# Input rows through another buffer ring, first sums' slabs loaded earlier, and two first-gate products in general PSUM banks

## The chip, the cores and the metric

The kernel runs on one core of a Trainium2 chip. The core has five instruction queues that run at their own pace and meet through semaphores: TensorE (PE, matrix products, which accumulate in eight PSUM banks), VectorE (DVE), ScalarE (ACT), GpSimd (POOL) and SyncE (SP, which here only issues transfers). Each queue executes in order. Sixteen DMA engines move data between main memory and the on-chip SBUF. The metric is the device time of one execution, in microseconds (us); lower is better.

## The reference, cut to what matters

One layer of a streaming encoder over 2048 prompt rows and 64 sample rows of width 1024, all in fp32. The first half of the layer makes two mixers, a convolution module and a chunk-band attention. The part that matters here begins behind them:

```python
merged = jax.nn.sigmoid(g_conv) * conv_out + jax.nn.sigmoid(g_attn) * attn_out
x = x + gt1 * (merged @ p['w_o'])

h2 = rms_norm(x, p['norm2_g']) * (1 + sc2) + sh2
gate, up = jnp.split(h2 @ p['w_ffn_in'], 2, axis=-1)
x = x + gt2 * ((jax.nn.silu(gate) * up) @ p['w_ffn_out'])
```

The FFN has 22 groups of 128 hidden columns; `w_ffn_in` holds the 22 gate groups and then the 22 up groups.

## The kernel before, in words

**Products.** An fp32 operand is kept as a high and a low part. For weights, ACT copies the slab into `whi` (rounded), and DVE or POOL subtracts, `wlo = slab - whi` ("the split"). A product is then three passes on PE: high by high, low by high, high by low (`mm3`).

**Blocks.** The second phase (merge, output projection, residual, FFN) goes over three blocks of tokens, `CBLOCKS`: 0 to 576, 576 to 1344, 1344 to 2112. The tokens of a block are cut into two halves of columns (288 in block 0, 384 in the others), and its FFN input `h2`, transposed, is held as four quarters b11, b21, b12, b22 (row half, column half of the tokens) and combinations t1 to t4 of them.

**Seven products.** The gate and the up weights of a group are combined in the manner of Strassen, so that seven quarter products do the work of eight. The weights' side needs four sums s1 to s4 of quarters of the gate's slab and of the up's slab. POOL makes them (`operand`, tiles named `ws`, a ring of four in SBUF), in the first block only, and each is stored to main memory (`sum_d`) for the blocks that follow. The names `g`, `u` in `operand` are the two slabs. `presum` makes a gate's sums ahead of their split. The splits of these weights run in the order of use.

**The start of a block's FFN.** Behind the output projection (PSUM tiles `pw`) runs `residual`, once per tile of 128 tokens (of 64 for the sample rows), as a generator that a planner steps: it loads the input rows `x_t` (two halves of 512 columns, in the ws ring too), adds them (`x1`), stores x1, takes the sum of squares on ACT, the root `r` on POOL, scales (`xn`, ACT), transposes on PE into `pw` or `pt` banks, scales the columns on DVE and ACT, and then makes the copies and differences: b11 and b21 for tokens of the first half, and for tokens of the second half t3, b22, t2, t1 and t4, each as a high copy on ACT and a low difference on DVE.

While the second half's tokens go through this, PE has work that needs the first half alone: the first five gates (`EARLY = 5`) use a plain product of b11 and b21 for the gate of the first half (`first(f)` and `second(f)`, ACT and DVE then make the silu of it, tiles `early` and `tg`). The first four products go into the banks that have the tags y0, z0, y1, z1; four more banks have the tag gp and serve in turn. Then follow the 22 groups (`up`), with products named by their weights' side, s1 to s4, a12, a22, and their tokens' side, t1 to t4, b21, b22; the early part of each ends in the tiles `u` and `v` on DVE.

**What sets the order.** `Stream` keeps a rough clock per engine as the program is written out, and calls deferred steps when its clock of PE has reached them: loads, splits, sums, generators. `Weights` walks a list of keys in the order of use (`weight_order`); what must come from main memory is listed in `items`, and `due` is the order of loading. A slab goes into the first of the classes wst (three buffers), wup and wfo that has room; a new load is issued on SP when a buffer comes free (`drop`, `left`). `get` makes what is not yet there. The framework then orders each engine's instructions, so that the order of PE around `first` and `second` is not literally the source's.

**Three lines hold the sums back.** In block 0 `W.hold` is true from the merge until the residual's column scalings are done; while it is, `presum` makes no sums, and `available` gives no key of kind `up` to the splits. And `presum` looks only at the key that is next to be split, `i = len(self.ready)`; as long as first-gate slabs (`fi`) are still to be split, it makes nothing.

In the profile nearly all instructions carry line 102, that of `Meter.run`, a helper which counts every operation; so the rows are told apart by the names of tiles. L1748 is the loading of x_t, L1767 the store of x1, L375 the load of a slab, L423 the store of a sum, L501 the store of a split first-gate slab.

Of the kernel before, what the change touches and what calls it, by code (L numbers as in the profile page):

```python
# [8 lines left out]
F32 = mybir.dt.float32  # L9
# [7 lines left out]
P = 128  # L17
D = 1024
# [9 lines left out]
FFN = 2816  # L28
# [235 lines left out]
class Weights:  # L264
# [5 lines left out]
    def __init__(self, engines, pool, dram, stream, keys, source, staging, held, kept):  # L270
# [2 lines left out]
        self.pool, self.dram, self.keys, self.source = pool, dram, keys, source  # L273

        self.staging, self.held, self.reach = staging, held, 0
        self.sum_pool, self.sum_d, self.sums, self.hold, self.landed = None, None, {}, 0, {}
        self.behind = nullcontext

        self.room, self.leaving = {"wst": 1, "wup": 0, "wfo": 0}, {"wst": 0, "wup": 0, "wfo": 0}
        times, raws = {}, {}  # L280
# [7 lines left out]
        for i, key in enumerate(keys):  # L288
            n = times[key] = times.get(key, 0) + 1
# [31 lines left out]
        self.due = {kind: [] for kind in self.tags}  # L321
        for i, key in enumerate(self.items):
            self.due[self.kind(key)].append(i)
        self.load_on("")

    @staticmethod
# [116 lines left out]
    def presum(self):  # L443

        i = len(self.ready)
        if not self.hold and i in self.first and all(self.landed.get(j, 1e18) <= self.stream.load["pe"] for j in self.need[i]):
            for f, op in self.keys[i][1:]:
                if op[0] == "s":
                    self.operand(f, op)
# [60 lines left out]
    def available(self):  # L510
        i = len(self.ready)
        if i >= len(self.keys):
            return False
        if i in self.need:
            if not self.there(i) or self.hold and self.keys[i][0] == "up":
                return False
            return True
        return self.keys[i] in self.stored

    def fill(self):  # L520
# [91 lines left out]
def streaming_layer(ctx: ExitStack, tc: tile.TileContext, I, O):  # L612
    nc = tc.nc
    stream = Stream()
    pe, dve, act, gps = (
        Meter(e, n, stream) for e, n in ((nc.tensor, "pe"), (nc.vector, "dve"), (nc.scalar, "act"), (nc.gpsimd, "pool"))
    )
    x_p, x_s = I["x_prompt"][0], I["x_sample"][0]
# [9 lines left out]
    def rows(prompt, sample, t, n):  # L628
        return prompt[t - SMP : t - SMP + n] if t >= SMP else sample[t : t + n]
# [137 lines left out]
    wk = p1.enter_context(tc.tile_pool(name="wk", bufs=1))  # L767
# [353 lines left out]
    def quarter(name, i, dtype=F32R, shape=(P, 4, CW // 2)):  # L1121

        return (wc, wk)[i].tile(list(shape), dtype, tag=f"half{i}", name=name, bufs=(4, 10)[i])
# [492 lines left out]
    W = Weights((nc.sync, act, dve, gps), wpool, dram, stream, list(weight_order()), source, 3, 5, lambda key: key[0] in KEPT)  # L1616
# [70 lines left out]
    wk = ctx.enter_context(tc.tile_pool(name="wk2", bufs=1))  # L1687
# [54 lines left out]
    def residual(pp, t, n, gt1, a, half, hs, free, last, i):  # L1742


        which = int(t < SMP)
        x_t = [wk.tile([P, 512], F32, tag="ws", name="x_t", bufs=4) for _ in range(2)]
        for j in range(2):
            nc.sync.dma_start(x_t[j][:n], rows(x_p, x_s, t, n)[:, 512 * j : 512 * j + 512])  # L1748
        yield
        x1 = token_row("x1")  # L1750
        for j in range(2):
            f = slice(512 * j, 512 * j + 512)
# [6 lines left out]
        for j in range(2):  # L1759
            f = slice(512 * j, 512 * j + 512)  # L1760
# [33 lines left out]
        for c, e, o in ((0, min(n, half - a), a), (max(0, half - a), n, max(0, a - half))):  # L1794
# [16 lines left out]
            t = pts[1][:, :, c:e]  # L1811
# [24 lines left out]
    for s, (lo, hi) in enumerate(CBLOCKS):  # L1836
# [4 lines left out]
        for i, (c0, c1) in enumerate(chunks):  # L1841
# [8 lines left out]
            if not groups:  # L1850
# [1 line left out]
                    gt1[which] = gt_row(0, which)  # L1852
                hs = {x: [quarter(x, 0) for _ in range(2)] for x in ("b11", "b21")}
                hs["rows"] = hs["columns"] = len(tiles)
            W.hold = not s

            def free():
                if xs:
# [9 lines left out]
            ws = {}  # L1868
# [44 lines left out]
        def bank(tag):  # L1913
            return bank_of(tag, "ps")[:, :half]
# [313 lines left out]

        def first(f):
            w = W.get(("fi", f * P))  # L2230
            x = bank(("y0", "z0", "y0", "z1", "y1")[f])
            product(x, [t[:, :4] for t in w], "b11", True, False)
            copy(early[f][0][:, :half], x)
            begin[f] = w, x
# [8 lines left out]
            step(f)  # L2243
        while hs["columns"]:
            turns.step(turns.gens[0])
        W.hold = False
        W.presum()
        if not s:
            W.begin_last()
# [19 lines left out]
        ws = [W.get(("fo", f)) for f in last]  # L2269
# [40 lines left out]
```

## Time and profile before

| | before |
|---|---|
| runs (us) | 2962.74, 2967.28, 2965.84 |
| median (us) | 2965.84 |
| the profiled execution's own time (us) | 2961.11 |
| its span (us) | 2959.3 |
| mean granted clock of TensorE | 0.996 |
| PE busy | 2888.9 us, 98% |
| DVE, ACT, POOL busy | 69%, 46%, 39% |

The profiled execution is one of several and took 4.7 us less than the median. Its span begins with the first and ends with the last instruction that the trace shows; 1.8 us lie around it. Times in the trace are counted from the start of the span. A row of the timeline gives the start, the duration, the engine, line and operation, then the tiles as out<-in with their shapes, the count of merged instructions, and in brackets the idle time of the engine before the first of them with the one that ended it. [...] The start of block 0's FFN lies at 1280 to 1360 us, that of block 1 at about 1830 to 1870, that of block 2 at about 2460 to 2500.

### The profile page before, as it was taken

To read this page: it belongs to the slowest core of one execution; us is meant where nothing else is said; L and a number is where in the kernel's file an instruction comes from. 1 tells how busy PE (TensorE), PEld (TensorE's weight loads), DVE (VectorE), ACT (ScalarE), POOL (GpSimd) and SP (SyncE) were. 2 spreads that over 40 slices of the span, in tenths; PEclk is the share of its full clock that TensorE was granted. 3 is DMA by queue.
4 is the path that set the end of the run, shared out by engine and by line. 5 is a ranking of instruction groups with operands and counts; after the bars stand their busy time and mean duration, and the time that the engine had idled before them with its cause. 6 is when DMAs were issued, how large, how long until landed. Compare 5 with 4: busy or idle time off the path is not lost.

```text
span 2959.3 us, 44845 instructions
## 1 busy us (share of the span) xinstructions
PE 2888.9 (98%) x16181; PEld 2583.0 (87%) x16181; DVE 2048.2 (69%) x3664; ACT 1365.8 (46%) x2453; POOL 1153.5 (39%) x745
## 2 busy tenths in 40 slices
PE   7999899999999999989999999999999999999999
PEld 5899777787888788879999999999999999999998
DVE  5897687668857885477777746676666547566666
ACT  3345633661465357464443345444444345444442
POOL 1101310111011102444466452366666742465767
PEclk9999999999999999999999999999999999999999
DMA  9989889988986888885444776332333975333333
GB/s 320 315 288 301 279 279 300 284 262 275 304 277 224 282 254 280 272 290 167 151 153 147 257 256 230 103 115 94 112 121 108 323 231 185 97 98 109 115 107 125
DMA packets 467724, 628.05 MB, mean 212 GB/s; under 512 B 36276, under 2 KB 314664, under 8 KB 467501
## 3 DMA queue, kind: packets, MB, share of 16 engines
q1 hardware_dynamic: 453600, 606.11, 63.1%
q10 hardware_dynamic: 13901, 19.08, 1.8%
q8 instruction: 127, 2.08, 0.3%
q14 instruction: 96, 0.79, 0.1%
HBM read 476.53 MB, written 148.54 MB: 211 GB/s over the span
## 4 chain that ended last, share of the span: by engine, by line
PE 82%; DVE 8%; DMA 4%; ACT 2%; POOL 2%; issue 2%; SPq 0%; ACTq 0%; POOLq 0%; DVEq 0%
PE ps L102 53%; PE pd L102 15%; PE pw L102 6%; DVE y L102 2%; PE sc L102 2%; PE po L102 2%; PE ptp L102 2%; DVE wlo L102 1%; PE pt L102 1%; PE pa L102 1%; ACT whi L102 1%; DMA tg<-g_d 1%; POOL wlo L102 1%; DVE pw L102 1%; DMA kk<-k_d 1%
## 5 line engine op out<-in xcount | busy, mean ns | idle before, releaser
L102 PE MATMUL ps<-t,whi 128*128 128x384 f32 (+1 forms) x2112 | 503.0, 322 | 9.0 <-ACT t L102 5.0
L102 POOL TENSOR_TENSOR wlo<-wst,whi 128x1024 fp32r<-128x1024 f32 (+1 forms) x159 | 363.6, 2297 | 249.4 <-ACT whi L102 227.1
L102 ACT ACTIVATE whi<-wst 128x1024 fp32r<-128x1024 f32 (+1 forms) x263 | 256.8, 979 | 321.0 <-PE ps L102 118.7
L102 PE MATMUL ps<-b,whi 128*128 128x384 f32 (+1 forms) x1584 | 380.6, 325 | 6.9 <-DVE early L102 3.6
L102 PEld LDWEIGHTS ps<-t,whi 128*128 128x128 f32 x2112 | 367.7, 188 | 17.0 <-ACT t L102 5.2
L102 DVE SCALAR_TENSOR_TENSOR y<-u,wd,y 128x512 f32<-128x512 f32 (+1 forms) x480 | 369.0, 773 | 6.3
L102 PE MATMUL ps<-hh,whi 128*128 128x512 f32 (+2 forms) x992 | 361.5, 364 | 0.0
L102 DVE TENSOR_TENSOR acc<-acc,pd 128x512 f32<-128x512 f32 x482 | 322.3, 684 | 49.6 <-PE pd L102 47.1
L102 PE MATMUL ps<-hl,whi 128*128 128x512 f32 (+2 forms) x992 | 345.6, 348 | 0.0
L102 PE MATMUL ps<-hh,wlo 128*128 128x512 f32 (+2 forms) x992 | 345.0, 348 | 0.0
L102 PE MATMUL ps<-t,wlo 128*128 128x384 f32 (+1 forms) x1056 | 339.2, 321 | 0.8 <-POOL wlo L102 0.7
L102 PE MATMUL pd<-whi,hid 128*128 128x512 f32 x912 | 297.0, 390 | 0.1
L102 PEld LDWEIGHTS ps<-b,whi 128*128 128x128 f32 x1584 | 277.8, 189 | 13.1 <-DVE early L102 4.5
L102 POOL TENSOR_TENSOR r<-t,mhalf 128x1 f32<-128x1 f32 (+2 forms) x68 | 84.4, 1243 | 445.3 <-DVE t L102 435.0
L102 PE MATMUL ps<-b,wlo 128*128 128x384 f32 (+1 forms) x792 | 256.6, 324 | 0.0
L102 ACT ACTIVATE pr<-pr,sm 128x640 f32<-128x640 f32 (+3 forms) x272 | 200.1, 747 | 111.0 <-DVE sm L102 108.5
L102 PEld LDWEIGHTS ps<-hh,wlo 128*128 128x128 f32 x992 | 186.7, 188 | 21.7
L102 PEld LDWEIGHTS ps<-hh,whi 128*128 128x128 f32 x992 | 187.1, 189 | 18.6 <-issue 1.6
L102 PEld LDWEIGHTS pd<-whi,hid 128*128 128x128 f32 x912 | 171.1, 188 | 35.6 <-ACT hid L102 0.7
L102 PEld LDWEIGHTS ps<-hl,whi 128*128 128x128 f32 x992 | 187.5, 189 | 15.5 <-issue 1.4
L102 PEld LDWEIGHTS ps<-t,wlo 128*128 128x128 f32 x1056 | 198.1, 188 | 2.4 <-POOL wlo L102 1.3
L102 PE MATMUL ps<-cin,whi 128*128 128x384 f32 (+2 forms) x768 | 184.0, 325 | 3.3 <-DVE o_p L102 1.4
(228 smaller groups left out, 6234.5 us busy)
## 6 DMA issues: line engine op xcount, KB each, us to landing
whi<-w_din_h SPq DMA_DIRECT2D x72, 512.0 KB, 6.8
wlo<-w_din_l SPq DMA_DIRECT2D x72, 512.0 KB, 7.4
wst<-sum_d SPq DMA_DIRECT2D x132, 256.0 KB, 2.9
wfo<-in_w_ffn_out SPq DMA_DIRECT2D x64, 512.0 KB, 3.4
wmod<-in_w_ada SPq DMA_DIRECT2D x46, 512.0 KB, 9.0
sum_d<-ws SPq DMA_DIRECT2D x88, 256.0 KB, 2.1
wst<-in_w_ffn_in SPq DMA_DIRECT2D x84, 256.0 KB, 3.2
wst<-in_w_in SPq DMA_DIRECT2D x40, 512.0 KB, 7.6
```

The costliest lines, as they stand in the source:

```text
L102: self.last = f(*args, **kw)
```

## The change

Four edits.

1. In block 0 (`W.early`, set where `W.hold` was), `residual` loads x_t as one tile of 1024 columns in the ring `half1` (ten buffers of 4 KB a partition, which also holds the quarters t1 to t4 and b22), not as two tiles in the ws ring. Blocks 1 and 2 keep the ws ring.
2. `W.hold` is gone: keys of kind `up` may be split, and sums may be made, whenever their slabs are there. `presum` also skips over the first-gate keys that are still to be split, and so can make the first `up` key's sums before them.
3. In the order of loading, the two slabs of gate 0's sums (`raws[0]`, `raws[FFN]`) are moved ahead of the fourth first-gate slab, `("fi", 3 * P)`.
4. `first(3)` and `first(4)` take gp banks and no longer z1 and y1. This holds for all blocks.

```diff
+        due = self.due[""]
+        for c in (0, FFN):
+            due.remove(raws[c])
+            due.insert(due.index(self.need[keys.index(("fi", 3 * P))][0]), raws[c])
         self.load_on("")
...
     def presum(self):
 
         i = len(self.ready)
-        if not self.hold and i in self.first and all(self.landed.get(j, 1e18) <= self.stream.load["pe"] for j in self.need[i]):
+        while i < len(self.keys) and self.keys[i][0] == "fi":
+            i += 1
+        if i in self.first and all(self.landed.get(j, 1e18) <= self.stream.load["pe"] for j in self.need[i]):
...
         if i in self.need:
-            if not self.there(i) or self.hold and self.keys[i][0] == "up":
-                return False
-            return True
+            return self.there(i)
...
-        x_t = [wk.tile([P, 512], F32, tag="ws", name="x_t", bufs=4) for _ in range(2)]
-        for j in range(2):
-            nc.sync.dma_start(x_t[j][:n], rows(x_p, x_s, t, n)[:, 512 * j : 512 * j + 512])
+        if W.early:
+            x_t = quarter("x_t", 1, F32, (P, D))
+            nc.sync.dma_start(x_t[:n], rows(x_p, x_s, t, n))
+            x_t = [x_t[:, 512 * j : 512 * j + 512] for j in range(2)]
+        else:
+            x_t = [wk.tile([P, 512], F32, tag="ws", name="x_t", bufs=4) for _ in range(2)]
+            for j in range(2):
+                nc.sync.dma_start(x_t[j][:n], rows(x_p, x_s, t, n)[:, 512 * j : 512 * j + 512])
...
-            W.hold = not s
+            W.early = not s
...
         def first(f):
             w = W.get(("fi", f * P))
-            x = bank(("y0", "z0", "y0", "z1", "y1")[f])
+            x = bank(("y0", "z0", "y0", "gp", "gp")[f])
             product(x, [t[:, :4] for t in w], "b11", True, False)
             copy(early[f][0][:, :half], x)
...
         while hs["columns"]:
             turns.step(turns.gens[0])
-        W.hold = False
         W.presum()
```

In the built order of PE, block 0's `first(3)` and `first(4)` stand ahead of the first product of gate 0 that uses t3; on POOL three of gate 0's sums stand between the splits of the first and the third first-gate slab; the count of PE instructions is the same, and up to the residual of block 0 so is their order.

More of the change, by code (lines that the diff above doesn't have):

```diff
@@ L275, in __init__ @@
         self.staging, self.held, self.reach = staging, held, 0
[L276 removed]
+        self.sum_pool, self.sum_d, self.sums, self.early, self.landed = None, None, {}, False, {}
         self.behind = nullcontext
```

## The prediction

> **What bounds the kernel now.** The page first: busy times, then the chain that ended last.
>
> ```profile
> span 2959.3 us, 44845 instructions
> PE 2888.9 (98%) x16181; PEld 2583.0 (87%) x16181; DVE 2048.2 (69%) x3664; ACT 1365.8 (46%) x2453; POOL 1153.5 (39%) x745
> ...
> PE 82%; DVE 8%; DMA 4%; ACT 2%; POOL 2%; issue 2%; SPq 0%; ACTq 0%; POOLq 0%; DVEq 0%
> ```
>
> TensorE (PE) is busy 98% of the span, so only its idle places can pay. The waits of PE in the stretch that the change rebuilds, the start of the first block's FFN, and then the same waits in block 1 (block 2's rows are the same):
>
> ```profile
> PE ps L102 <- ACT t L102: 5.0, 1, 5.0
> PE ps L102 <- DVE early L102: 2.6, 1, 2.6
> PE ps L102 <- DVE u L102: 1.6, 1, 1.6
> PE ps L102 <- DVE v L102: 1.4, 1, 1.4
> ```
>
> ```profile
> PE ps L102 <- DVE early L102: 0.5, 1, 0.5
> PE ps L102 <- DVE v L102: 0.4, 1, 0.4
> PE ps L102 <- POOL wlo L102: 0.3, 1, 0.3
> ```
>
> That is 10.6 us in block 0 and 1.2 in each later block: 0.4% of the time is at stake in all. Two rows of the timeline of PE show the last two places (start, duration, in brackets the idle time before and who ended it), and three rows of the table of stretches what DVE did there (columns: length, then busy us of PE, PEld, DVE, ACT and POOL with their instructions, granted clock, DMA share, GB/s).
>
> ```profile
> 1312.42 0.58 PE L102 MATMUL ps<-t,whi 128*128 128x288 f32 x1 [4.99 <-ACT t L102]
> ...
> 1328.50 0.54 PE L102 MATMUL ps<-t,whi 128*128 128x288 f32 x2 [1.61 <-DVE u L102]
> ```
>
> ```profile
> 1302.00:1313.00 11.00, 4.38 (x27) 3.90 (x28) 11.00 (x23) 9.63 (x23) 1.41 (x2) 0.98 1.03 398
> 1312.00:1316.00 4.00, 3.58 (x15) 3.58 (x16) 4.00 (x8) 1.68 (x4) 3.30 (x3) 0.57 0.68 244
> 1316.00:1328.00 12.00, 10.79 (x79) 10.18 (x77) 12.00 (x16) 6.18 (x13) 5.57 (x4) 1.00 0.57 177
> ```
>
> The reader is to see that PE has the holes but DVE is full: 11.00 of 11, 4.00 of 4, 12.00 of 12. This stretch ends when DVE has made gate 0's u, at 1328.44; PE's next matmul is at 1328.50. The timeline of DVE over it:
>
> ```profile
> 1301.42 1.08 DVE L102 TENSOR_TENSOR wlo<-ws,whi 128x512 fp32r<-128x512 f32 x1 [5.18 <-ACT whi L102]
> 1302.42 0.41 DVE L102 TENSOR_SCALAR pw<-pw,A,B 128x128 f32<-128x128 f32 x1
> ...
> 1304.43 0.68 DVE L102 TENSOR_TENSOR wlo<-ws,whi 128x512 fp32r<-128x512 f32 x1
> ...
> 1320.40 1.55 DVE L102 TENSOR_TENSOR wlo<-ws,whi 128x512 fp32r<-128x512 f32 x1
> ...
> 1326.32 1.76 DVE L102 TENSOR_TENSOR wlo<-ws,whi 128x512 fp32r<-128x512 f32 x1
> 1328.00 0.44 DVE L102 TENSOR_TENSOR u<-ps,early 128x288 f32<-128x288 f32 x1
> ```
>
> From 1301.42 no row of DVE has an idle time: 27.0 us of work, after 5.18 us in which it stood for the copy of the first sums. Those are made by POOL:
>
> ```profile
> 1286.95 2.55 POOL L102 TENSOR_TENSOR wlo<-wst,whi 128x512 fp32r<-128x512 f32 x2 [2.19 <-ACT whi L102]
> 1292.34 2.54 POOL L102 TENSOR_TENSOR wlo<-wfo,whi 128x512 fp32r<-128x512 f32 x2 [2.84 <-ACT whi L102]
> 1295.01 0.55 POOL L102 TENSOR_TENSOR r<-t,mhalf 128x1 f32<-128x1 f32 x1
> ...
> 1296.84 1.29 POOL L102 TENSOR_TENSOR ws<-wst 128x512 f32<-128x512 f32 x1
> ...
> 1311.51 1.27 POOL L102 TENSOR_TENSOR ws<-wst 128x512 f32<-128x512 f32 x1 [9.56 <-DMA sum_d<-ws]
> ```
>
> **The change part by part.**
>
> *Input rows in the ring.* Ten loads of 256 KB become five of 512 KB: the same bytes, five issues of SP fewer (0.94 / 2, about 0.5 us each). Three of the five no longer wait for a ws buffer and go out between 1234 and 1244, ahead of weight slabs. SP's timeline and the stretch:
>
> ```profile
> 1235.65 0.94 SPq L1748 DMA_DIRECT2D x_t<-in_x_prompt  x2
> ```
>
> ```profile
> 1235.00:1262.00 27.00, 26.78 (x189) 24.43 (x188) 16.76 (x40) 19.78 (x33) 20.63 (x11) 1.00 0.76 240
> ```
>
> I cost this at nothing: the slabs behind them still wait for their buffers, the DMA engines are busy 0.76 there, and PE 26.78 of 27. If that cover were gone, a load is 512 KB at 398 GB/s, 1.3 us: three of them, 4 us at most; no gain is to be had.
>
> *First sums when landed, their two slabs ahead.* In the built order three of gate 0's four sums stand on POOL ahead of the split of the third first-gate slab (the row at 1286.95). They need a slab that takes the place of this one (SP's timeline; DMA issues, with the time to landing):
>
> ```profile
> 1282.39 0.37 SPq L375 DMA_DIRECT2D wfo<-in_w_ffn_in  x1
> ```
>
> ```profile
> wfo<-in_w_ffn_in SPq DMA_DIRECT2D x1, 512.0 KB, 4.2
> ```
>
> So they run from 1287.0 (1282.4 + 0.4 + 4.2) to 1290.9 (3 x 1.29). The split behind them comes 3.9 later, POOL's idle 2.84 ahead of the next takes most of it, and r comes 1.1 later, at 1296.1. ACT meanwhile copies two of the sums, 0.63 each, before it scales xn, which it did here:
>
> ```profile
> 1295.96 1.14 ACT L102 ACTIVATE xn<-x,r 128x1024 f32<-128x1024 f32 x1
> ```
>
> That covers r; xn is done at 1298.3, 1.2 later. PE's transposes of it follow, some of them behind the 12 matmuls of second(0) at 0.14 (10.79 us for 79): DVE can scale the columns from about 1300.5, where it began at 1302.42. The two halves of gate 0's first split (1.08 + 0.68 = 1.76 us) now lie in DVE's idle 5.18 us. What is left of the 27.0 us is 25.3, so without a stall u would be there at 1325.8, 2.6 us earlier.
>
> But stalls come in. The fifth first-gate slab has lost its place to the sums' and is issued at SP's next such row, 1286.09. It lands 4.2 later (the load above) to 7.6 later (the next load of this kind behind it, in the full window): 1290.7 to 1294.1.
>
> ```profile
> 1286.09 0.38 SPq L375 DMA_DIRECT2D wst<-in_w_ffn_in  x1
> ```
>
> ```profile
> wst<-in_w_ffn_in SPq DMA_DIRECT2D x1, 512.0 KB, 7.6
> ```
>
> ```profile
> 1291.63 1.15 ACT L102 ACTIVATE whi<-wfo 128x512 fp32r<-128x512 f32 x2 [0.16 <-PE pw L102]
> ```
>
> ACT copies it at 1291.63 (last row), and behind that copy stand the sums of squares and the scaling of xn. In the middle, at 1292.4, it is 0.8 late; that much is taken up below, where DVE waits 1.0 in t4 and t2; at 1294.1 it would cost 1.5 more. Gate 1's sums cannot move: they need the ws buffers of gate 0's sums, free when these are stored. That store let POOL go at 1311.51 after 9.56 us, and it will again, because the DMA engines are full (1.03, 398 GB/s) with the same bytes in the same order as after the change. And in the built order ACT now has the copies of gate 1's sums ahead of the copies t4, t2 and t1 of the second phase's residual. Before, they stood so:
>
> ```profile
> 1313.57 0.60 ACT L102 ACTIVATE t<-pw 128x512 fp32r<-128x512 f32 x1 [1.20 <-DVE pw L102]
> 1314.16 0.63 ACT L102 ACTIVATE whi<-ws 128x512 fp32r<-128x512 f32 x1
> ```
>
> After: three sums of 1.28 from 1311.5, done 1312.8, 1314.1, 1315.4; the third copy ends 1316.0, t4's copy 1316.6, t2's 1317.8. Walking DVE's new list with the durations above I find it waiting 1.3 us for ACT in the scaling (ACT has a third copy, of 0.63, and two more early steps to fit in), 1.0 at t2 of tile 0 (five ACT copies queue ahead), 0.4 at t4, 0.6 at t2 of tile 1: 3.3 us. So u is there at 1325.8 + 3.3 = 1329.1, +0.6 against before; bounds -2.6 (no stall) and +3.4 (the copies one sum, 1.3, later, and the 1.5 of the late slab).
>
> *Fourth and fifth first gates in general banks.* In before, one matmul of gate 0 (`ps<-t`, at 1312.42) stands ahead of first(3) and waits 4.99 us for t3, and all first gates' products behind it wait too. Now they come first and fill the 2.6 and much of the 4.99. That is no gain in itself: PE executes in order and all of it ends at u. What PE no longer has to do between u's operands and u is four more `t` matmuls, 4 x 0.14 = 0.5 us; the rest of the filled holes comes back as waiting for t3, t2 and u. I take -0.5, bounds 0 and -1.6, the whole wait at 1328.50.
>
> The third hole, `v`, is other work (PE's timeline, then DVE's):
>
> ```profile
> 1359.67 0.53 PE L102 MATMUL ps<-b,whi 128*128 128x288 f32 x2 [1.39 <-DVE v L102]
> ```
>
> ```profile
> 1355.59 3.66 DVE L102 TENSOR_TENSOR wlo<-ws,whi 128x512 fp32r<-128x512 f32 x3 [8.56 <-ACT whi L102]
> ```
>
> v stood behind three splits that ran beside POOL's sums. In the new order gate 2's v comes ahead of the second half of that split. I take -1.0; bounds 0 and -1.4.
>
> *The same banks in blocks 1 and 2.* There first(3) and first(4) take a bank that a tile of the residual holds until DVE has read it (DVE's timeline).
>
> ```profile
> 1850.44 0.68 DVE L102 TENSOR_TENSOR pw<-b,pw 128x512 f32<-128x512 f32 x1
> ...
> 1852.99 0.69 DVE L102 TENSOR_TENSOR t<-pw,t 128x512 fp32r<-128x512 f32 x1
> ```
>
> By the new order PE reaches them 0.4 and 0.25 before these reads end (1851.1, 1853.7), against the 0.3 for POOL's wlo that goes. I take +0.3 a block, +0.6 together; bounds -0.6 (the 0.3 twice, no new wait) and +2.8 (each of four waits one DVE operation of 0.69).
>
> **Sum:** +0.6 - 0.5 - 1.0 + 0.6 = -0.3 us on the profiled execution's 2961.1 (span 2959.3, 1.8 around it), which is 4.7 below the median of the runs shown, 2965.84. I carry it to the median: 2965.5. About 0.2%, 5.9 us, is what a measurement of this kernel can tell from no change.
>
> [...] The clock: after the stall of 4.99 us the granted clock is 0.57 in 1312 to 1316, and a matmul took 0.24 us (3.58 for 15) where it takes 0.14 in the next row (10.79 for 79): 15 x 0.10 = 1.5 us, which DVE covered. [...]
>
> **The rivals.**
> 1. *DVE comes free and most of the holes go.* The splits that ran beside a sum on POOL took 1.55 and 1.76 instead of 0.68. If the new order keeps them apart, these two save 1.55 + 1.76 - 2 x 0.68 = 1.95 us, and two between them, taken at 0.65 each, bring it to 3.3; with -2.6 (no ACT stall), -0.5, and -1.4 at v: -7.8, with the later blocks +0.6, -7.2, so 2958.6. For it: DVE is the whole chain there. Against: in the new order POOL's later sums stand between the same splits. [...]
> 2. *Slower: the stores hold ACT.* One mechanism: the copies of gate 1's sums on ACT, now ahead of t4, t2, t1, inherit POOL's 9.56 us wait for the stores. Each microsecond that the stores land after 1311.5 makes u one later. From landing at 1317 on it decides the verdict; at 1319 to 1320, +8: 2973.5. For it: the full DMA engines; the late fifth slab adds to it. Against: the bytes ahead of the stores are the same.
> 3. *Nothing moves.* The slabs land too late for the sums to go ahead, and the order falls back: 2965.8. For it: the slab issued at 1282.39 lands as the DMA engines fill. Against: the sums are due at 1287, when it has landed; a microsecond or two is all that they have.
>
> **How the numbers follow.** My forecast, within a few microseconds of before, 0.40, its own range 2962 to 2969 (most of the way to the bounds of u, v and the later blocks: -3.5 to +3.5); rival 3, 0.08; rival 1, 0.28; rival 2 (with loads that come late before 1262, up to 4 us, as a lesser form), 0.24. Rival 1 counts as faster, rival 2 as slower, the rest as the same: 0.28, 0.48, 0.24. The range for all, 2956 to 2974, leaves out the ends of the two rivals, about 1 in 10 each.
>
> **What would show it.** Right: the 2.6 and 4.99 before 1313 are gone from PE's waits, a wait for t3 or t2 stands in 1309 to 1319, and u is still within 2 us of 1328.4 on DVE; POOL's sums at 1287 to 1291, and gate 1's still after a wait for sum_d; ACT's row of t4 behind a copy of ws. The v row at 1359 is short. Blocks 1 and 2 show a wait of a first-gate product for DVE at about 1851 and 1853. Wrong: u at 1323 or earlier (rival 1), or after 1334 (rival 2); a PE wait over 1 us before 1262; PE waits in blocks 1 and 2 of over 2 us each.

## The result, and the profile after

The changed kernel takes 2971.47 us (median of 20 runs, 2966.1 to 2977.06), the kernel before 2964.84 (20 runs on the same chip, 2962.57 to 2975.89). The ratio is 1.0019, 95% interval 1.0013 to 1.0025: slower, by 5.6 us on 2965, between 3.9 and 7.4 (the medians themselves differ by 6.6). The forecast was 2965.5, no change.

The profile page of the changed kernel, span, busy times and the chain that ended last:

```profile
span 2965.7 us, 44829 instructions
...
PE 2893.8 (98%) x16181; PEld 2585.2 (87%) x16181; DVE 2053.0 (69%) x3663; ACT 1364.9 (46%) x2453; POOL 1157.8 (39%) x746
...
PE 79%; DVE 8%; DMA 6%; ACT 3%; issue 2%; POOL 2%; SPq 1%; ACTq 0%; POOLq 0%; DVEq 0%
```

The span is 6.4 us longer, and PE is busy 4.9 us longer with the same number of matmuls: some of them ran slower. The share by engine does not tell where. So a ruler is needed, and PE gives one: both programs issue 16181 matmuls. The n-th of them marks the same progress in both traces, whatever the local order, and the distance between two marks is the length of a stage. Marks that matter: matmul 7093 (1280.1 us in before) to 7927 (1428.1) holds the start of block 0's FFN; 10360 to 10581 (1840 to 1880) that of block 1; 13626 to 13859 (2466 to 2508) that of block 2. Worked out so from the start times:

| stage (us) | before | after | difference |
|---|---|---|---|
| block 0, start of the FFN | 148.02 | 152.02 | +4.00 |
| block 1, start of the FFN | 39.90 | 40.93 | +1.03 |
| block 2, start of the FFN | 42.12 | 43.14 | +1.02 |

Together +6.05 of the span's +6.4. The other eleven stages into which I cut the traces differ by 0.35 or less, the time ahead of the first of them (1184 us) by 0.9.

PE's waits in the first of these stages of the changed kernel (1280.8 to 1432.7; us in total, times, longest):

```profile
PE ps L102 <- DVE hid L102: 2.7, 1, 2.7
PE ps L102 <- DVE t L102: 2.2, 2, 1.9
PE ps L102 <- DVE u L102: 2.0, 1, 2.0
PE ps L102 <- DVE early L102: 1.8, 1, 1.8
PE ps L102 <- ACT early L102: 1.4, 2, 0.9
PE ps L102 <- ACT t L102: 1.0, 1, 1.0
PE ps L102 <- DVE v L102: 0.6, 1, 0.6
PE ps L102 <- ACT whi L102: 0.6, 1, 0.6
```

The 4.99 and 2.63 are gone and v's 1.39 is 0.6; in their place stand six waits of 0.3 to 1.9 between 1310 and 1322, u's is longer (2.0 against 1.6), and hid's 2.7 is new. Two more rows, from the table of stretches, show PE behind the wait for u (columns as in the prediction: length, busy us of PE with its matmuls, then the other engines, granted clock, DMA share, GB/s). First the changed kernel, where the wait for u ends at 1330.52, then before, where it ends at 1328.50:

```profile
1321.40:1327.40 6.00, 5.90 (x26) 5.90 (x27) 6.00 (x10) 1.64 (x3) 4.36 (x3) 0.53 0.44 161
...
1330.50:1334.00 3.50, 3.48 (x15) 3.50 (x16) 2.65 (x5) 0.00 (x0) 0.91 (x1) 0.52 0.82 243
```

```profile
1328.40:1332.40 4.00, 3.90 (x29) 3.90 (x30) 3.04 (x7) 0.56 (x1) 1.40 (x2) 1.00 0.83 230
```

15 matmuls in 3.48 us against 29 in 3.90: behind u, where every lost microsecond counts, PE now runs at half clock, and it did not before.

The work in front of u and hid is on DVE and POOL. DVE in front of u, and in front of hid; then POOL:

```profile
1324.13 2.50 DVE L102 TENSOR_TENSOR wlo<-ws,whi 128x512 fp32r<-128x512 f32 x2
...
1326.92 1.41 DVE L102 TENSOR_TENSOR wlo<-wst,whi 128x512 fp32r<-128x512 f32 x1
1328.25 1.75 DVE L102 TENSOR_TENSOR wlo<-ws,whi 128x512 fp32r<-128x512 f32 x1
1329.92 0.45 DVE L102 TENSOR_TENSOR u<-ps,early 128x288 f32<-128x288 f32 x1
...
1339.22 2.49 DVE L102 TENSOR_TENSOR wlo<-ws,whi 128x512 fp32r<-128x512 f32 x1
```

```profile
1312.55 1.26 POOL L102 TENSOR_TENSOR ws<-wst 128x512 f32<-128x512 f32 x1 [11.84 <-DMA sum_d<-ws]
...
1322.88 1.51 POOL L102 TENSOR_TENSOR ws<-wfo,ws 128x512 f32<-128x512 f32 x1 [6.47 <-ACT t L102]
1324.47 1.61 POOL L102 TENSOR_TENSOR ws<-wst 128x512 f32<-128x512 f32 x1
1326.16 1.62 POOL L102 TENSOR_TENSOR ws<-ws,wup 128x512 f32<-128x512 f32 x1
1327.74 1.71 POOL L102 TENSOR_TENSOR ws<-wup,wst 128x512 f32<-128x512 f32 x1
...
1338.76 2.40 POOL L102 TENSOR_TENSOR wlo<-wfo,whi 128x1024 fp32r<-128x1024 f32 x1
```

Four sums run back to back on POOL from 1322.88 to 1329.45, and the four splits beside them on DVE take 2.50 + 1.41 + 1.75 = 5.66, where one alone takes 0.68: about 2.9 too much. But before has the same at this place. Beside the rows of 1.55 and 1.76 that the prediction shows stand these:

```profile
1322.84 1.78 DVE L102 TENSOR_TENSOR wlo<-ws,whi 128x512 fp32r<-128x512 f32 x2
...
1324.90 1.49 DVE L102 TENSOR_TENSOR wlo<-wst,whi 128x512 fp32r<-128x512 f32 x1
```

Five splits take 1.55 + 1.78 + 1.49 + 1.76 = 6.58 there, about 3.2 more than five alone. So the stretched splits delay u in both kernels, and they are not what makes it later in the changed one.

What is new is on the way to hid. At 1338.76 POOL splits the second slab of `w_ffn_out`, which DVE splits in before, and the split beside it on DVE takes 2.49; hid stands behind that.

### The profile page after: what moved, and what is told of

Its sections match the earlier page's. It is cut to its first block, busy times and chain, and to the rows that moved or that the text cites. A ratio compares the mean times of both kernels' runs of the same rounds, so it can differ in the third digit from the quotient of the medians.

```text
span 2965.7 us, 44829 instructions
## 1 busy us (share of the span) xinstructions
PE 2893.8 (98%) x16181; PEld 2585.2 (87%) x16181; DVE 2053.0 (69%) x3663; ACT 1364.9 (46%) x2453; POOL 1157.8 (39%) x746
## 4 chain that ended last, share of the span: by engine, by line
PE 79%; DVE 8%; DMA 6%; ACT 3%; issue 2%; POOL 2%; SPq 1%; ACTq 0%; POOLq 0%; DVEq 0%
PE ps L102 51%; PE pd L102 15%; PE pw L102 5%; DVE y L102 2%; PE po L102 2%; PE sc L102 2%; PE ptp L102 2%; DVE wlo L102 1%; ACT whi L102 1%; PE pt L102 1%; DMA wmod<-in_w_ada 1%; DMA tg<-g_d 1%; PE pa L102 1%; DMA kk<-k_d 1%; POOL r L102 1%
## 5 line engine op out<-in xcount | busy, mean ns | idle before, releaser
L102 DVE TENSOR_TENSOR acc<-acc,pd 128x512 f32<-128x512 f32 x482 | 322.5, 685 | 49.8 <-PE pd L102 47.2
L102 DVE TENSOR_TENSOR wlo<-wst,whi 128x1024 fp32r<-128x1024 f32 (+1 forms) x106 | 132.0, 1247 | 82.0 <-ACT whi L102 80.8
```

Source lines behind the costliest of these rows:

```text
L102: self.last = f(*args, **kw)
```

## The experiments

All times of runs are ratios to the kernel before on the same chip. They resolve about 3 us (0.1%), so most readings go by the stage. For block 0's stage there are two more numbers, worked out from PE's start times: *waits*, by how much the matmuls that start after idle time come later than the usual distance (0.132 us for 288 columns); and *slow*, the same for matmuls that follow without idle time but over 0.03 late. What is left is 130.1 to 130.7 in every kernel (131.8 in filler, which has 12 matmuls more). Each row is one profiled execution; the ratio is over all runs.

| kernel | block 0 | waits | slow | block 1 | ratio, 95% interval |
|---|---|---|---|---|---|
| before | 148.02 | 13.2 | 4.3 | 39.90 | 1 |
| after | 152.02 | 15.0 | 6.8 | 40.93 | 1.0019, 1.0013 to 1.0025 |
| after_again | 153.58 | 14.0 | 9.3 | 40.92 | 1.0017, 1.0005 to 1.0029 |
| gp_alone | 148.94 | 12.4 | 6.3 | 40.93 | 1.0009, 0.9999 to 1.0018 |
| no_gp | 146.59 | 12.7 | 3.5 | 39.94 | 0.9996, 0.9986 to 1.0006 |
| gp_first | 153.99 | 16.9 | 6.9 | 39.92 | 1.0013, 1.0004 to 1.0023 |
| fo_dve | 148.90 | 12.8 | 6.0 | 40.91 | 1.0011, 1.0001 to 1.0022 |
| act_order | 153.16 | 13.9 | 9.0 | 40.96 | 1.0016, 1.0007 to 1.0025 |
| one_input | 146.61 | 12.4 | 4.1 | 40.96 | 1.0003, 0.9994 to 1.0013 |
| no_gp_due | 148.88 | 14.0 | 4.2 | 39.94 | 1.0007, 0.9998 to 1.0016 |
| all3 | 148.00 | 10.5 | 7.3 | 39.91 | 0.9996, 0.9988 to 1.0005 |
| u_first | 150.84 | 14.9 | 5.7 | 40.92 | 1.0015, 1.0006 to 1.0024 |
| all3_u | 145.85 | 9.3 | 6.4 | 39.94 | 0.9997, 0.9988 to 1.0005 |
| nogp_u | 149.89 | 14.1 | 5.2 | 39.94 | 1.0013, 1.0004 to 1.0022 |
| filler | 149.59 | 12.3 | 5.5 | 40.95 | 1.0024, 1.0014 to 1.0034 |
| before_one | 146.84 | 11.7 | 4.5 | 39.93 | 1.0001, 0.9990 to 1.0012 |
| gp_alone_one | 144.31 | 9.6 | 4.6 | 40.92 | 0.9994, 0.9984 to 1.0004 |
| no_gp_one | 145.59 | 11.8 | 3.3 | 39.90 | 0.9988, 0.9978 to 0.9997 |

**How well a stage repeats.** The changed kernel, unedited, once more.

> The changed kernel once more, for how well a stage's length repeats from one profiled execution to the next. Block 0's stage within 0.5 us of 152.0, the later blocks within 0.1 of 40.93 and 43.14, the waits for t3, early, u and hid each within 0.2.

Blocks 1 and 2 repeat (40.92, 43.13). Block 0 does not: the waits for hid and u are 2.1 and 1.8 (2.7 and 2.0 the first time), and yet the stage is 1.56 us longer, because slow matmuls take 2.5 more. There is a third stretch of half clock, behind the wait for hid; the three of this execution, from the table of stretches:

```profile
1322.00:1328.20 6.20, 6.20 (x26) 6.20 (x27) 6.20 (x9) 1.64 (x3) 4.67 (x3) 0.51 0.48 170
1331.00:1334.90 3.90, 3.87 (x18) 3.90 (x19) 3.26 (x6) 0.00 (x0) 0.92 (x1) 0.56 0.84 237
1344.90:1348.60 3.70, 3.68 (x16) 3.69 (x17) 2.64 (x8) 1.14 (x3) 1.28 (x1) 0.54 0.64 198
```

So a difference of block 0 under some 1.6 us between two single executions is not a reading, and the half clock is the term that does not repeat.

**The banks alone.** Before, with edit 4:

```diff
-            x = bank(("y0", "z0", "y0", "z1", "y1")[f])
+            x = bank(("y0", "z0", "y0", "gp", "gp")[f])
```

> The kernel before with edit 4 alone: first(3) and first(4) in general banks, in all blocks; loads, sums and hold as before. Theory (the loss of the changed kernel is 4 us in block 0, from DVE, ACT and the clock, and 1 us in each later block, from the banks): blocks 1 and 2 each 1.0 us longer than before, block 0 within 1 us of before, since gate 0's u on DVE stays at about 1328 and PE's filled holes come back as waits; in all +1 to +3 us. Rival (the banks cost nothing, the later blocks are longer for another reason): blocks 1 and 2 as before, in all 0.

The later blocks are those of the changed kernel, +1.03 each: they come from the banks alone. Block 0 is +0.9, within what repeats, but its make-up is the new one: less waiting (-0.8), more half clock (+2.0), 23 matmuls in the 4.60 us from 1330.60 at a granted clock of 0.63.

**All but the banks.** The changed kernel with the old line above.

> The changed kernel without edit 4: first(3) and first(4) in z1 and y1 again. Theory: blocks 1 and 2 as before; block 0 still 2 to 4 us longer, with u at about 1330 and the second w_ffn_out slab's split on POOL beside a DVE split of over 2 us; PE's stall of about 5 us for t3 is back. In all +2 to +4 us. Rival (block 0's loss comes from PE's new order): block 0 as before, in all 0.

The expectation fell: block 0 is 1.4 us shorter than before (within what repeats), not longer, and u is there 46.3 after the first mark (48.3 before, 49.6 after). PE's waits, and the stretch behind the wait for u:

```profile
PE ps L102 <- ACT t L102: 5.7, 1, 5.7
...
PE ps L102 <- DVE u L102: 0.8, 1, 0.8
```

```profile
1327.20:1331.20 4.00, 3.92 (x29) 3.92 (x30) 3.40 (x7) 0.57 (x1) 1.08 (x1) 1.00 0.81 230
```

One long wait, far in front of u, and full clock behind u. The early sums do no harm, and neither edit accounts for the +4.0: it comes when both are together.

**Banks in block 0 only.**

```diff
+            x = bank((("y0", "z0", "y0", "z1", "y1") if s else ("y0", "z0", "y0", "gp", "gp"))[f])
```

> The changed kernel with the general banks in block 0 only. Theory: 2 us less than the changed kernel, that is +3.5 to +4 us against before, blocks 1 and 2 as before, block 0 as in the changed kernel. Rival (banks cost nothing in the later blocks): the same as the changed kernel, +5.5.

Blocks 1 and 2 return to 39.92 and 42.15, block 0 stays bad. The two losses are separate.

**The second slab's split on DVE**, in block 0 (`split`):

```diff
             late = key[0] in ("up", "fo") and ...
+            late = late or self.early and key == ("fo", 1)
```

> The changed kernel with the split of the second w_ffn_out slab of block 0 on DVE, where the kernel before has it, not on POOL. Theory (POOL's split of 2.4 us stretches a DVE split that runs beside it from 0.7 to 2.5 us, which leads to PE's stall of 2.70 us at 1345 for DVE's hid): that stall is under 0.5 us, and the time 2 to 2.7 us less than the changed kernel, +3 to +3.5 against before. Rival (the stall follows from u being late, whoever splits): the stall stays over 2 us and so does the time, +5.5.

PE's waits for u and hid, and DVE's two splits of `w_ffn_out`:

```profile
PE ps L102 <- DVE u L102: 2.4, 1, 2.4
...
PE ps L102 <- DVE hid L102: 0.6, 1, 0.6
```

```profile
1336.53 2.30 DVE L102 TENSOR_TENSOR wlo<-wfo,whi 128x1024 fp32r<-128x1024 f32 x1
...
1339.55 1.52 DVE L102 TENSOR_TENSOR wlo<-wfo,whi 128x1024 fp32r<-128x1024 f32 x1
```

The wait for hid falls from 2.7 to 0.6, and the stage by 3.1. DVE does the slab itself in 1.52, and POOL now has the split of ws that took DVE 2.49 in front of hid (2.26 on POOL, at 1339.95). So the wait comes from who makes which split there; the run moves two splits at once, and does not part the stretching from the order.

**ACT's order.** ACT's copies of gate 1's sums, ahead of t4, t2 and t1 in the changed kernel, are queued behind the copies of t3, t2 and t1, DVE's and POOL's order as they were:

```diff
+    def queue_act(self, key):
+        late = self.early and key[0] == "up" and key[-1][0] == 1 and self.tail
+        return self.issue_after(self.tail) if late else nullcontext()
...
-            self.act.activation(hi[:, c], src, AF.Copy)
+            with self.queue_act(key):
+                self.act.activation(hi[:, c], src, AF.Copy)
...
             split(*at("t1"), b[0])
+            W.tail = act.last.ins
```

> The changed kernel; the copies on ACT of gate 1's sums (and of the last of gate 0) are queued behind the copies of t3, t2 and t1, and not ahead of them. DVE's and POOL's order stay as they were. Theory (ACT's order is one part of the late u): the two idle places of DVE for t on ACT (0.64 and 0.31 us at 1317.6 and 1318.6) go, and u comes about 1 us earlier, 48.6 after the landmark of 1280 (49.6 in the changed kernel, 46.3 without the banks), the stage about 1 us shorter, 151; the stall for hid stays at 2.7. Rival (ACT's order is all of it): u at 46 to 47, the stage 148.5 to 149. Rival (DVE has the same work in front of u and fills the time elsewhere): u stays at 49.3 to 49.9, the stage 152. Time 2967 to 2970 by the theory.

u came at 48.2, 1.4 earlier, as the theory had it. But the stage did not get shorter. PE's waits and the two stretches behind them:

```profile
PE ps L102 <- DVE hid L102: 3.0, 1, 3.0
PE ps L102 <- DVE u L102: 2.4, 1, 2.4
```

```profile
1331.20:1335.20 4.00, 3.96 (x30) 3.96 (x31) 3.76 (x7) 0.62 (x1) 1.42 (x2) 1.00 0.80 230
1344.50:1350.80 6.30, 6.28 (x24) 6.03 (x25) 3.98 (x10) 2.40 (x6) 1.28 (x1) 0.51 0.72 215
```

Here a wait of 2.4 is followed by full clock and one of 3.0 by 24 matmuls at half. ACT's queue, on which much of the prediction's sum was spent, is worth 1.4 us at u and does not by itself make the stage longer.

**POOL's sums beside DVE's splits.** The sums of gates 1 to 3 in block 0 become copies of their first input. All orders stay.

```diff
-                self.gps.tensor_tensor(t, x, y, e)
+                if f in (1, 2, 3):
+                    self.gps.tensor_copy(t, x)
+                else:
+                    self.gps.tensor_tensor(t, x, y, e)
```

> The changed kernel; the sums of gates 1 to 3 on POOL (block 0) are copies of their first input, an instruction with one input in SBUF and not two, so these gates' sums are wrong values; all orders stay. Theory (a sum with two inputs on POOL stretches the split with two inputs beside it on DVE): the splits of ws and wst in front of u, which took 2.50 for two, 1.41 and 1.75, take 1.3, 0.7 and 0.7, so u comes up to 3 us earlier (46.7 to 48 after the landmark), and the stage gets as much shorter, 149 to 150. The split on POOL that made hid late has two inputs still, so the 2.7 us for hid stay. Rival (any instruction of POOL on SBUF does it, or the splits are long for another reason): they stay over 1.2 us each and u at 49 to 50; if the copies are shorter than 1.29, then u comes earlier by that alone, under 1 us.

The same splits on DVE in front of u, and a copy on POOL:

```profile
1325.73 1.30 DVE L102 TENSOR_TENSOR wlo<-ws,whi 128x512 fp32r<-128x512 f32 x2
...
1327.32 0.73 DVE L102 TENSOR_TENSOR wlo<-wst,whi 128x512 fp32r<-128x512 f32 x1
1327.97 1.09 DVE L102 TENSOR_TENSOR wlo<-ws,whi 128x512 fp32r<-128x512 f32 x1
```

```profile
1327.46 1.07 POOL L102 COPY ws<-wup 128x512 f32<-128x512 f32 x1
```

The splits take 3.1 and not 5.7, u comes at 45.4, 4.2 earlier, PE's wait for it is 0.5 and not 2.0, and the stage is 5.4 shorter. The wait for hid stays, at 2.0 (2.7 in after). The experiment does not tell one input from a shorter instruction: a copy takes 0.62 alone and not 1.29, and beside it a split is still stretched (1.09, and the copy to 1.07). What in the two instructions makes them slower side by side is not shown.

**Is that the whole difference?** The same replacement in before, in gp_alone and in no_gp.

> The kernel before, with the sums of gates 1 to 3 on POOL as copies of their first input (one input in SBUF, 0.62 us and not 1.29; those gates' values are wrong), all orders as before. In the changed kernel that made block 0's stage 5.4 us shorter (152.0 to 146.6). Theory (POOL's sums beside DVE's splits are the whole difference between the two kernels in block 0): here the stage, 148.0, becomes only 1 to 2 us shorter, 146 to 147, so that the two kernels with these copies lie within 0.7. Rival (the edits lose time in block 0 in another way also): the stage falls by as much as in the changed kernel, to 142.5 to 144.5, and a difference of over 2 us is left between the two.

> The kernel before with the general banks alone, and the copies in place of the sums of gates 1 to 3. Its stage was 148.9. By the theory 146 to 147.2, by the rival under 145.5.

> The changed kernel without the general banks, and the copies in place of the sums of gates 1 to 3. Its stage was 146.6. By the theory the four kernels (edits 1 to 3, edit 4, both, none) lose the interaction of +4.5 us that they have with the real sums (148.0, 146.6, 148.9, 152.0): this one 144.5 to 146.3, and what both together cost over the two apart is under 1.2 us. By the rival the interaction stays over 2.5 us: this one under 143.5 or before's over 147.

before_one and no_gp_one lie where the theory had them, gp_alone_one does not. Without the banks the replacement is worth 1.2 (before) and 1.0 (no_gp), with them 4.6 (gp_alone) and 5.4 (after). With the copies, before and after are equal (146.84, 146.61), as the theory said. But what the edits cost together beyond the two apart, 4.5 with the sums (152.02 - 148.94 - 146.59 + 148.02), is still 3.5 with the copies (146.61 - 144.31 - 145.59 + 146.84), where under 1.2 was expected. So the stretching of splits beside POOL's sums sits in all four kernels, and in these executions more of it shows with the banks.

PE's marks say where most of this interaction sits. Of the four kernels with the sums only after waits for hid (2.86 by the marks), and of the four with the copies only one_input (2.2), since the copies leave the splits of the slabs as they were. In no_gp POOL has that split too, of 2.41, but there DVE makes hid ahead of its split of wst, in after behind it, and PE does not wait. The other part is chance: behind the same wait of 2.63 before_one ran at half clock and lost 1.2, and before did not; without it, the 1.2 that the copies are worth in before would be some 2.4. Less these two terms, the 3.5 is about 0.2, and the 4.5 less hid is 1.6, as much as two executions of one program differed by. That POOL's sums are the whole difference between the two kernels is not shown; the wait for hid is the larger part of what the edits cost together. Each of the terms is a single execution.

**Where the slabs' order comes in.** no_gp without edit 3, the old order of loading.

> The changed kernel without its edits 3 and 4: the input rows in the other ring, the sums free to be made when landed, but their slabs in the old order of loading, and the old banks. Theory (what made block 0 shorter by 1.4 us without the banks is that sums are made early, in POOL's and DVE's idle time at 1287 to 1301, which needs the slabs ahead): the block's stage is as before, 147.5 to 149, u at 47.8 to 49 after the landmark, the later blocks 39.9 and 42.1. Rival (it is the ring or the freed order): 146 to 147 as with edit 3. Time 2963 to 2966.

148.88 against no_gp's 146.59, u at 48.7 against 46.3: the gain without the banks needs the slabs ahead, as the theory had it, by a difference somewhat over what repeats.

**Gate 1's splits behind u on DVE**, in the changed kernel, in one with gp_first, act_order and fo_dve together (all3), and in no_gp:

```diff
+    def behind_u(self, key, name):
+        late = name == "dve" and self.u and self.early and key[0] == "up" and key[1][0] == 1
+        return self.issue_after(self.u) if late else nullcontext()
...
-            e.tensor_tensor(lo[:, c], src, hi[:, c].bitcast(F32), ALU.subtract)
+            with self.behind_u(key, name):
+                e.tensor_tensor(lo[:, c], src, hi[:, c].bitcast(F32), ALU.subtract)
...
             keep(u2, y)
+            if W.no_u:
+                W.no_u, W.u = False, dve.last.ins
+                W.fill()
```

> The changed kernel; in block 0 the four splits of gate 1's weights, which DVE made in front of gate 0's u (beside POOL's sums, 2.50 us for two, 1.41 and 1.75), are queued behind u. Theory (these splits, stretched by POOL, set u): u is ready as soon as PE has its product, 1.4 us earlier or more, 46.5 to 48.3 us after the landmark of 1280 (49.6 in the changed kernel), and PE's wait for u is under 0.6; the stage is 1.5 to 3 us shorter, 149 to 150.5. The splits behind u then meet POOL's sums there, so a wait of gate 1's products for whi or wlo of up to 1 us may come. Rival (DVE's work is the same, and what is moved behind u makes v, hid or gate 1's split late by as much): the stage 151.5 to 152.5. Time 2968 to 2971 by the theory.

> The changed kernel with three repairs: general banks in block 0 only, ACT's copies of gate 1's sums behind the copies of t, and the second slab of w_ffn_out split on DVE in block 0. Theory (the losses found so far are separate and add up): later blocks 39.9 and 42.1 as before (-2.0 against the changed kernel), the stall for hid 0.6 or less (-2.1), u about 1 us earlier; the stage of block 0 147.5 to 149.5, the time 2963 to 2966. Rival (the order of splits on DVE is what matters, and each repair shifts it): block 0 over 150 all the same, 2967 or more.

> The kernel with three repairs (general banks in block 0 only, ACT's copies of gate 1 behind those of t, second slab of w_ffn_out split on DVE), and gate 1's splits behind u on DVE. Theory: it had a wait of 3.80 us for u with 2.76 us of half clock behind it; u now comes when PE has its product, up to 3.5 us earlier, the wait is under 0.8, and with it the half clock goes or moves ahead of u: the stage 143.5 to 146 instead of 148.0, the time 2960 to 2963, faster than both kernels. Rival (the splits are only moved): 147 to 149, the time as before.

> The changed kernel without the general banks, and with gate 1's splits behind u on DVE. Without the banks u came at 46.3, and PE waited only 0.82 for it, so by the theory at most 0.8 is to be had there: u at 45.5 to 46.3, the stage 145.5 to 146.6, the time 2961 to 2963. Rival: the splits moved behind u make gate 1's products wait: 147 to 148.5.

In u_first u is there at 43.6, 6 us earlier, and PE starts again at nearly the same place, 49.4 (49.8 in the changed kernel). DVE, then PE:

```profile
1323.56 0.45 DVE L102 TENSOR_TENSOR u<-ps,early 128x288 f32<-128x288 f32 x1
...
1325.88 1.78 DVE L102 TENSOR_TENSOR wlo<-wst,whi 128x512 fp32r<-128x512 f32 x1
1327.59 1.76 DVE L102 TENSOR_TENSOR wlo<-ws,whi 128x512 fp32r<-128x512 f32 x1
1329.27 0.45 DVE L102 TENSOR_TENSOR v<-ps,early 128x288 f32<-128x288 f32 x1
```

```profile
1329.86 0.51 PE L102 MATMUL ps<-t,whi 128*128 128x288 f32 x2 [1.69 <-DVE v L102]
```

The stage, 150.84, lies between the two forecasts; in the mechanism the rival held: the stretched splits now stand in front of v, and PE waits for v. nogp_u says the same, by more than the rival had (149.9, with a wait of 3.0 for v). DVE's work, stretched by POOL, sets the end of this stretch in both orders. all3 brings block 0 back to before's length and the later blocks too, and adds up as expected; all3_u is 2.2 shorter still, against an expected 2 to 4.5, and little over what repeats. In the runs both are as fast as before, no more; so is no_gp. No version that makes all the sums was shown to be faster than the kernel before.

**Matmuls in the wait.** PE makes gate 0's product of s2 and t2 twice in the changed kernel.

```diff
+                with tc.issue_after(pe.last.ins):
+                    product(bank("y1"), w2, "t2", True, True)
```

> The changed kernel; in block 0, PE makes gate 0's product of s2 and t2 a second time, into a free bank that nobody reads, behind the first time: 12 matmuls, 1.6 us at full clock, in place of most of PE's wait for u of 2.05. The work of the other engines up to u stays as it was. Theory (the half clock behind u, 14 matmuls and 1.58 us, comes from the idle time right in front of u): u stays at 49.6, the wait for it is 0.5 or less, the matmuls behind u take 0.13 and the stage is 1.2 to 1.8 us shorter, 150.2 to 150.8. Rival (the half clock follows the idle time of 1312 to 1321 at a fixed distance, or lasts a given time): the matmuls behind u still take 0.24, and the stage is 152 or, if the added product itself runs at half clock and delays u's own product, up to 153.5.

Inconclusive on the clock. The scheduler moved gate 1's first products behind the wait, so PE still stood 2.6 us in front of u, and 16 matmuls at half clock followed. The stage, to the same last matmul and with the 12 added, is 149.6, but not by the mechanism expected: the wait for hid went.

## Why the prediction was wrong

It forecast -0.3 us, and the profiled execution shows +6.0 in the three stages. Block 0's +4.0 by PE's marks: the restart behind u +1.36, the slow matmuls behind it +1.24, the wait for hid +2.86, v -0.78, the end of the stage -0.22, the rest -0.46. The steps that failed are three: hid was left out (+2.86), filled holes were said to cost nothing (the half clock, +1.24), and the short waits of the later blocks were mis-sized (+2.05 for +0.6). Nearly all the signs of being right came true all the same, since none of them looked at hid, at the clock behind u, or closely at the size of the short waits.

1. *Input rows in the ring: nothing.* Right: the stage ahead of block 0's is 95.84, and 96.09 in before.
2. *First sums when landed: u +0.6, between -2.6 and +3.4.* The steps came: sums at 1286.92 to 1290.8, the fifth slab late on ACT, gate 1's sums after 11.84 us for the store, and the copies of t behind three copies of sums. u was 1.3 later on DVE, inside the bounds, but by luck: the errors on the way cancel. Two rows of DVE in the changed kernel:

```profile
1291.65 2.69 DVE L102 TENSOR_TENSOR wlo<-wup,whi 128x512 fp32r<-128x512 f32 x2 [0.19 <-ACT whi L102]
...
1302.76 0.42 DVE L102 TENSOR_SCALAR pw<-pw,A,B 128x128 f32<-128x128 f32 x1 [1.50 <-PE pw L102]
```

   Counted from the first mark (0.66 later in this trace), the scaling of columns began 0.3 earlier than before, where the sum had 1.9: a split at 1291.65, beside POOL's, took 2.69 and not 1.29, and the fifth slab kept ACT until 1293.81, both ahead of xn. From there to u DVE is busy 26.0 us in both traces, where the sum had 25.3, and it waits 1.6 for ACT (0.64, 0.64 and 0.31), where the sum had 3.3. So -0.3 and +1.6 make the 1.3. The walk used durations of the old trace for the splits; but the splits of rival 1, which stayed beside the sums, are as long in before and explain no difference.
3. *The banks: -0.5, at most nothing.* The four matmuls fewer are there (0.64 by the marks, most of the rest of -0.46). What failed is the sentence that filling PE's holes "is no gain in itself": here it came with a loss. Before, PE had one long wait with half clock behind it, and u still to come as cover. With the banks the waits are many, and the last lie close to u. The slow term is 5.5 to 9.3 in the ten executions with these banks in block 0 and the real sums, and 3.5 to 5.2 in the four without. The prediction had such a cost behind the 4.99 alone, 1.5 us that DVE covered, and none in its sum, since no stall of that length was foreseen in front of u; the stall was 2.05 and the cost 1.24 (1.6 of half clock, less 0.3 that before had too).
4. *Nothing was said of hid: +2.86.* This is the largest single term, and it was left out altogether. hid stands between u and v, and the prediction went from the one to the other. POOL has the second split of `w_ffn_out` in the changed kernel, DVE in before; that edits move a split from one engine to the other was not asked.
5. *v: -1.0.* Right in kind and nearly in size: -0.78.
6. *Later blocks: +0.6.* The mechanism was right, gp_alone and gp_first show that the banks are the cause, the size was not: +2.05. The two waits that were foreseen came at their places (0.14 and 0.18), and a third, of 0.19, for ACT's early copy. The term that was mis-sized is the cost of a short wait. PE in block 1 of the changed kernel:

```profile
1853.00 0.62 PE L102 MATMUL ps<-b,whi 128*128 128x384 f32 x2 [0.19 <-ACT early L102]
...
1853.63 0.51 PE L102 MATMUL ps<-b,whi 128*128 128x384 f32 x2
...
1858.09 0.62 PE L102 MATMUL ps<-b,whi 128*128 128x384 f32 x2 [0.18 <-DVE t L102]
```

The idle time shown is counted from the end of the matmul before, and matmuls overlap: they start 0.174 apart and last 0.34. So a wait of 0.19 makes a start 0.35 late, and the first pair behind it takes 0.62 instead of 0.51, another 0.1. Each wait costs 0.26 beyond what its row shows. Three new ones (0.19, 0.14, 0.18), one gone (0.34) and two late matmuls at 1868 (0.34, at full clock) make 0.51 + 0.78 - 0.60 + 0.34 = 1.03.

Of the rivals, 2 gave the sign and not the mechanism: the stores let POOL go at 1312.55, one microsecond later than before and not five or more, and ACT was not what held the stage (act_order).

## What to carry to other kernels

Filling a hole of the bounding engine was not free here: one long wait that something else covered was cheaper than the same time in several short ones near the end of the stretch, since each restart cost 0.26 us beyond the wait that its row shows (block 1), and half clock followed windows of 3.41 us in which PE was busy 1.44 or less (the section below). Where two engines work side by side (a split of 0.68 us took 1.41 and 1.75 beside POOL's sums in the changed kernel), walk the *new* order with the durations of instructions that run side by side, not with those of the old trace. And walk it to the end of the stage without leaving out a step: the largest term stood between two that were looked at. Compare with before at the same place, too: a stretched split explains nothing if before has it as well.

## What was not expected of the hardware

Half clock came back after waits of 2.0 (after) and did not after one of 2.4 (act_order), and one program had two such stretches in one execution and three in the next. The length of the wait alone does not decide: up to the second of its stretches of half clock, at 1330, the changed kernel's stage had no wait over 2.05.

The clock that the traces record says more. In this stage before has one stretch at a granted clock of 0.50, 3.41 us from 1312.48; after has two, 6.83 us from 1320.20 and 3.41 from 1330.44, and the two starts lie 10.24 apart, three times 3.41. Counted on from such a stretch in windows of 3.41 us, the edges do not fall at the same place of the work in two executions. Two of these windows around the wait of 2.63, in before and then in before_one (columns as above):

```profile
1298.83:1302.24 3.41, 1.77 (x16) 1.54 (x14) 0.82 (x1) 1.48 (x4) 3.12 (x3) 1.00 1.07 387
1302.24:1305.65 3.41, 2.02 (x14) 1.77 (x14) 3.41 (x10) 3.32 (x10) 0.00 (x0) 1.00 1.04 422
```

```profile
1312.28:1315.69 3.41, 1.19 (x11) 0.95 (x9) 1.42 (x3) 2.08 (x5) 2.53 (x3) 1.00 1.08 389
1315.69:1319.10 3.41, 3.00 (x12) 3.00 (x13) 3.41 (x8) 2.20 (x7) 0.00 (x0) 0.50 1.03 420
```

The same wait lies across two windows in before, PE is busy 1.77 and 2.02 in them, and the clock stays; in before_one most of it lies in one, PE is busy 1.19, and the next window has half clock. In the same way PE is busy 1.44 in the window ahead of the restart behind u in after (half clock follows), and 2.04 and 2.36 in the two that share the wait of 2.4 in act_order (it does not). Six windows of after, the last with most of the wait of 2.70 for hid:

```profile
1316.79:1320.20 3.41, 1.33 (x4) 0.67 (x4) 2.46 (x5) 2.27 (x5) 0.00 (x0) 1.00 0.22 84
1320.20:1323.61 3.41, 2.11 (x9) 2.11 (x10) 3.41 (x7) 1.01 (x2) 0.73 (x1) 0.50 0.43 154
1323.61:1327.03 3.42, 3.42 (x16) 3.42 (x16) 3.42 (x6) 0.63 (x1) 3.26 (x3) 0.50 0.24 90
1327.03:1330.44 3.41, 1.44 (x11) 1.20 (x10) 3.41 (x4) 1.26 (x2) 2.73 (x3) 1.00 0.90 303
1330.44:1333.85 3.41, 3.33 (x14) 3.37 (x15) 2.56 (x5) 0.00 (x0) 0.97 (x1) 0.50 0.83 247
...
1340.68:1344.09 3.41, 1.59 (x13) 1.36 (x11) 3.41 (x5) 0.07 (x1) 1.75 (x2) 1.00 0.80 261
```

Over the whole stage, in before and after together, half clock followed three windows of full clock, with PE busy 0.06 (before, from 1309.07), 1.33 and 1.44; in all the other windows of full clock PE was busy 1.59 or more. Half clock went on behind the window with 2.11, and full clock came back behind those with 3.41 (before), 3.42 and 3.33. So in these traces half clock went with how the waits fell into the windows, and not with the length of one. That the edges lie elsewhere from one execution to the next is my reading of why one program had two such stretches in one execution and three in the next; what makes the windows and sets their edges was not shown.

A split of 128x512 on DVE, 0.68 us alone, takes up to 1.78 beside sums of the same size on POOL (u_first) and 2.49 beside a split of twice that size (after), and POOL's sum 1.5 to 1.7 in place of 1.29 (after): both lose.
